# Output projection of a hybrid attention layer: weight blocks split two blocks ahead across products, operand load buffers for each token group, rows of x asked for in products 6 and 4

## The chip, the cores and the metric

The kernel runs on one core of a Trainium2 chip. The metric is the device time of one execution in microseconds (us); lower is better. Times are medians of several runs; a profile is one further execution.

## What is computed

One step of a layer with two groups of heads. A combined input projection feeds stick-breaking attention (8 heads) and retention (8 heads); each branch is normalised by head and gated; both are joined and go through one output projection, and the normalised result is added to the input:

```python
h = rms_norm(x, norm_pre)
q_sb, k_sb, v_sb, gate_sb, q_r, k_r, v_r, gate_r = project(h, w_in, pos)
...
y = jnp.concatenate([y_sb, y_r], axis=-1)
out = jnp.einsum('bte,ed->btd', y, w_out)
xp = xp + rms_norm(out, norm_post)
```

There are 1024 prompt tokens and 8 x 16 = 128 sample tokens, a model width of 2048 and weights w_out of 2048 x 2048, all in float32. The change concerns only the last part, the product y w_out, its normalisation and the addition of x, which fills about the last 395 us.

## The kernel before, in words

**Tiling.** Tokens lie in tiles of 128. Group 0 holds prompt tiles 0 to 3 and the sample tile, group 1 prompt tiles 4 to 7. The output product of a group is done by Strassen's scheme: seven products n, each of a combination of token halves and width halves of y (table LEFT) and one of blocks of w_out (table RIGHT). The order is 5 for group 0 (still in the stage before), then 1, 2, 5 (for group 1 alone), 3, 6, 7, 4. Products 1, 2 and 3 also carry the sample tile in an ordinary product.

**A half product.** Each product has two halves, nh = 0 and 1, of 512 output columns; I call them 1a, 1b and so on. A half (product, L1182) runs over eight blocks k of 128 rows of the weights. Every float32 operand is split in two parts that TensorE takes at full rate: hi is a rounded copy (ScalarE, L162), lo the remainder (VectorE, L163), in the names wh and wl for weights, mh and ml or ah and al for tokens of group 0 and group 1, sh and sl for the sample. A block thus costs three matmuls (hi x hi, hi x lo, lo x hi; L1159, L1162, L1163) for each accumulator: five accumulators in 1, 2 and 3, four in 6, 7 and 4. In 1a the matmuls of group 1 run two blocks behind (LAG). PSUM has eight banks, in a ring; a half takes its four or five from it, the sample's last.

**Loading weights.** load_split (L1174) asks for a block on SyncE's queue into wr (five buffers), and splits it into wh and wl (four buffers each). In the code it stands at the head of iteration k.

**Other work beside the matmuls.** Generators called jobs are advanced by tick(), one step a tick, and a number of ticks follows each group of three matmuls: three for product 1, two for 6 and 7, one otherwise. Jobs are: left (L290), which loads eight pieces of y for each group and splits them into operands of the next product (buffers yr, four, one tag for both groups); left_sample (ys); sums (L271), which loads pieces of y for group 1 (br, two buffers), adds them on VectorE and stores them (s_s, issued by ScalarE); collect (L1206), which copies or adds finished accumulators into the result; complete (L1267), which squares and multiplies by the gain gpost; finish (L1295), which scales four pieces of a finished tile on ScalarE and lets GpSimd's queue add them onto the output rows, which hold x already. The list `then` says in which half the operands of which product are prepared, and they are drained before that product begins.

**The end.** In 4a the eight weight blocks of 4b are also loaded and split, into kept tiles (keep_blocks, L1358). 4b then runs one tile at a time, and its tiles add x themselves: rows of x (128 x 2048, 1 MB) are asked for in load_row (L1369).

**What sets the order.** Each engine runs its instructions in order. The program text gives the order within an engine roughly; a scheduler moves instructions by its own estimate of readiness, except that those that are pinned (pin, L180) may not pass the last matmul written ahead of them. Weight splits are not pinned; the jobs' steps are.

Of the kernel before, what the change touches and what calls it, by code (L numbers as in the profile page):

```python
# [2 lines left out]

# [6 lines left out]
F32 = mybir.dt.float32  # L10
# [6 lines left out]
P = 128  # L17
D = 2048
# [41 lines left out]
D_SUM2 = (4, 6, 36)  # L60
D_SUM3 = (2, 3, 6)
LAG = 2
HT = KT // 2
HALF = D // 2
KEPT = 5
D_KEEP = 2
# [21 lines left out]
def tile_hybrid_step(  # L88
# [27 lines left out]
    nc = tc.nc  # L116
# [12 lines left out]
    def x_rows(t):  # L129
        return x_prompt[0, t * P : (t + 1) * P, :] if t < PT else xs_flat  # L130
# [99 lines left out]
    def drain(job):  # L230
        while job is not None and not job.done:
            tick()
# [57 lines left out]
    def left(gi, n, hi, lo, bufs, tag, deep):  # L290
        src = LEFT[n]
        raw = []

        def load(h):
            r = bufs.tile([P, 256], F32, name=tag, tag=tag, bufs=deep)
            if src[0] == "y":
                pin(nc.sync.dma_start(r, s_y[gi][src[1] * H + h][:, src[2] * 256 : src[2] * 256 + 256]))
            else:
                pin(nc.sync.dma_start(r, s_s[gi][h][:, src[1], :]))
            raw.append(r)  # L300

        for h in range(deep - 1):
            load(h)
        yield D_OP
        for h in range(HT):
            if h + deep - 1 < HT:
                load(h + deep - 1)
            r = raw.pop(0)
            pin(*split(hi[h], lo[h], r))
            yield D_OP  # L310
# [125 lines left out]
    with ExitStack() as s1:  # L436
# [737 lines left out]
        def load_split(n, nh, k):  # L1174
            wr = wp.tile([P, 512], F32, name="wr3", tag="wr", bufs=5)
            nc.sync.dma_start(wr, weights_of(n, nh, k))
            wh = wp.tile([P, 512], F32R, name="wh3", tag="wh")
            wl = wp.tile([P, 512], F32R, name="wl3", tag="wl")
            split(wh, wl, wr)
            return wh, wl  # L1180

        def product(n, nh, groups, sample, ticks, upto=HT, feed=(), lag=0):  # L1182
            todo = [((g, p), bank(), mine[g, n], TS[p]) for g in groups for p in range(2)]
            if sample:
                todo.insert(2, ("s", bank(), mine["s", SAMPLE_LEFT[n]], TS[0]))
            blocks = []
            for k in range(upto + lag):
                if k < upto:
                    blocks.append(load_split(n, nh, k))
                next(iter(feed), None)  # L1190
                for key, a, x, ts in todo:
                    at = k - lag if key[0] == 1 else k
                    if 0 <= at < upto:
                        times(a, x, at, ts, *blocks[at], at == 0, at == HT - 1)
                        for _ in range(ticks):
                            tick()
            return [(key, a) for key, a, _, _ in todo]
# [40 lines left out]
    with ExitStack() as s3:  # L1238
# [18 lines left out]
        def tile_of(key):  # L1257
            return SAMPLE if key[1] == 4 else GROUPS[key[0]]["tiles"][key[1]]
# [48 lines left out]
        def both(n, groups):  # L1307
            made = []
            for g in groups:
                mine[g, n] = operand(c3, ("ah", "al"), 256, bufs=2) if g else kept(at[n])  # L1310
                made.append(left(g, n, *mine[g, n], rp, "yr", 4))
            return made

        def jobs_of(made):
# [2 lines left out]
        def all_of(made):  # L1317
# [5 lines left out]
            (1, 1): ((2, BOTH),), (2, 1): ((5, G1), (3, G0)), (5, 0): ((3, G1),), (3, 0): ((6, BOTH),),  # L1323
            (6, 0): ((7, BOTH),), (7, 0): ((4, BOTH),),
        }
        (first,) = both(1, G1)
        more = Job(sums(fp, [sum_rows(1, h) for h in range(H)], D_SUM3), 16)
        Job(load_gpost(), 40)
# [3 lines left out]
        for n, groups in ((1, BOTH), (2, BOTH), (5, G1), (3, BOTH), (6, BOTH), (7, BOTH)):  # L1332
            for nh in range(2):
                if n > 1 and nh == 0:
                    all_of(ready)
                    ready = []
                if (n, nh) == (2, 1):
                    drain(more)
                for what in then.get((n, nh), ()):
                    ready += jobs_of(both(*what))  # L1340
                start = dict(feed=first, lag=LAG) if (n, nh) == (1, 0) else {}
                accs = product(n, nh, groups, n < 4, {1: 3, 6: 2, 7: 2}.get(n, 1), **start)
                if (n, nh) == (2, 1):
                    phases.close()
                    xp.append(s3.enter_context(tc.tile_pool(name="xp", bufs=1)))
                Job(collect(n, nh, accs), 1)
# [2 lines left out]
        at_end = [half[1].rearrange("p a n -> p (a n)").rearrange("p (k n) -> p k n", k=KEPT) for half in mov]  # L1349
        rest = [mp.tile([P, HT - KEPT, 512], F32R, name=f"w{t}", tag=t) for t in ("mh2", "ml2")]  # L1350
        keep = [[x[:, k] for k in range(KEPT)] + [y[:, k] for k in range(HT - KEPT)] for x, y in zip(at_end, rest)]
        LAST = ((0, 0), (0, 1), (1, 0), (1, 1))
        rows = {
            key: pool.tile([P, D], F32, name=f"x{i}", tag=tag)
            for i, (key, pool, tag) in enumerate(zip(LAST, (rp, rp, xp[0], xp[0]), ("out0", "out1", "x2", "x3")))
        }

        def keep_blocks():  # L1358
            for k in range(HT):
                wr = wp.tile([P, 512], F32, name="wr3", tag="wr", bufs=5)  # L1360
                pin(nc.sync.dma_start(wr, weights_of(4, 1, k)))
                yield 1
                pin(*split(keep[0][k], keep[1][k], wr))
                yield D_KEEP
            for key in LAST[:2]:
                load_row(key)
                yield D_KEEP

        def load_row(key):  # L1369
            pin(nc.sync.dma_start(rows[key], x_rows(tile_of((key[0], 2 + key[1])))))  # L1370

        keeping = Job(keep_blocks(), 1)
        Job(collect(4, 0, product(4, 0, BOTH, False, 2)), 1)
# [1 line left out]
        scaled = [c3.tile([P, 2, 512], F32, name=f"og{t}", tag=t) for t in ("sh", "sl")]  # L1375
        for g, p in LAST:
            key = g, 2 + p
            if g == 0:
                load_row((1, p))
            a = bank()  # L1380
            for k in range(HT):
                times(a, mine[g, 4], k, TS[p], keep[0][k], keep[1][k], k == 0, k == HT - 1, k == 0)
                if (g, p) == (0, 0):
                    tick()
                    tick()
            if (g, p) == (0, 0):
                while jobs:
                    tick()
            o = area(key, 1)
            nc.vector.tensor_tensor(o, o, a, ALU.subtract)  # L1390
            square(key, 1, o)
            t = scaled[g][:, p, :]
            nc.vector.tensor_tensor(t, o, gpost[:, 512:1024], ALU.mult)
            rs = scale(key)
            for c in (0, 2, 3, 1):
                part = t if c == 1 else area(key, c)
                if c or (g, p) == (1, 1):
                    x = rows[g, p][:, c * 512 : (c + 1) * 512]
                    nc.vector.scalar_tensor_tensor(part, part, rs, x, ALU.mult, ALU.add)
                    store(key, c, nc.sync, part)  # L1400
                else:
                    nc.scalar.activation(part, part, AF.Copy, scale=rs)
                    add_out(key, c)
# [104 lines left out]
```

## Time and profile before

| | |
|---|---|
| median of 3 runs | 2335.07 us (2333.79 to 2336.39) |
| profiled execution, whole | 2337.12 us |
| its span, first to last instruction | 2335.4 us |
| granted TensorE clock, mean | 0.992 |
| halves 1a to 4a | 1977.9 to 2303.5 us |
| 4b, one tile after another | 2303.5 to 2325.3 us |

A row of the timeline gives the start in us, the length in us, the engine, the line, the operation with output and inputs, and in brackets how long the engine had been idle and what released it. A row of waits gives who waited for what, the total in us, how often, and the longest. In the rows all accumulators are called a.

### The profile page before, as it was taken

To read this page: it belongs to the slowest core of one execution; us is meant where nothing else is said; L and a number is where in the kernel's file an instruction comes from. 1 tells how busy PE (TensorE), PEld (TensorE's weight loads), DVE (VectorE), ACT (ScalarE), POOL (GpSimd) and SP (SyncE) were. 2 spreads that over 40 slices of the span, in tenths; PEclk is the share of its full clock that TensorE was granted. 3 is DMA by queue.
4 is the path that set the end of the run, shared out by engine and by line. 5 is a ranking of instruction groups with operands and counts; after the bars stand their busy time and mean duration, and the time that the engine had idled before them with its cause. 6 is when DMAs were issued, how large, how long until landed. Compare 5 with 4: busy or idle time off the path is not lost.

```text
span 2335.4 us, 39299 instructions
## 1 busy us (share of the span) xinstructions
PE 2273.8 (97%) x14496; PEld 2050.2 (88%) x14496; DVE 1234.1 (53%) x2541; ACT 920.5 (39%) x1951; POOL 356.9 (15%) x601
## 2 busy tenths in 40 slices
PE   7999999999999999999999999999999999899997
PEld 7999999999999999998888979888889887688775
DVE  7234444353435444355556565655665666545565
ACT  6323333333333333334343334333343445335362
POOL 3002020110202020111111202020220221000020
PEclk9999999999999999999999999999999999999999
DMA  7546657575557647577678787777876767835585
GB/s 253 175 147 201 192 151 218 177 208 172 172 173 206 196 150 220 177 203 253 163 235 213 229 223 229 225 211 228 237 226 204 209 171 200 273 126 168 140 181 189
DMA packets 446497, 462.61 MB, mean 198 GB/s; under 512 B 181984, under 2 KB 309984, under 8 KB 444640
## 3 DMA queue, kind: packets, MB, share of 16 engines
q1 hardware_dynamic: 315952, 295.69, 43.5%
q0 software_dynamic: 28720, 78.41, 11.9%
q10 hardware_dynamic: 101632, 86.00, 11.7%
q8 instruction: 113, 1.85, 0.3%
q14 instruction: 80, 0.66, 0.1%
HBM read 355.12 MB, written 114.29 MB: 201 GB/s over the span
## 4 chain that ended last, share of the span: by engine, by line
PE 83%; DMA 8%; DVE 5%; ACT 2%; issue 2%; SPq 1%; POOL 0%; DVEq 0%; ACTq 0%; POOLq 0%
PE acc L366 46%; PE accn L422 17%; PE a L1162 3%; PE a L1159 3%; PE a L1163 3%; PE pa L747 2%; PE z L717 2%; PE pd L850 1%; PE zc L786 1%; DMA mr<-s_h 1%; DMA yr<-s_y 1%; DMA ro<-s_rk 1%; DMA wr<-s_b 1%; DMA yr<-s_s 1%; DVE wl L163 1%
## 5 line engine op out<-in xcount | busy, mean ns | idle before, releaser
L366 PE MATMUL acc<-mh,wh 128*128 128x256 f32 (+2 forms) x2304 | 663.1, 340 | 0.0
L366 PE MATMUL acc<-ml,wh 128*128 128x256 f32 (+2 forms) x2304 | 659.3, 339 | 0.0
L366 PE MATMUL acc<-mh,wl 128*128 128x256 f32 (+2 forms) x2304 | 656.9, 338 | 0.0
L163 DVE TENSOR_TENSOR wl<-wr,wh 128x512 fp32r<-128x512 f32 x504 | 345.9, 690 | 495.8 <-ACT wh L162 463.7
L162 ACT ACTIVATE wh<-wr 128x512 fp32r<-128x512 f32 x504 | 316.5, 630 | 632.8 <-PE acc L366 342.5
L366 PEld LDWEIGHTS acc<-ml,wh 128*128 128x128 f32 x2304 | 421.7, 188 | 31.4 <-issue 3.3
L366 PEld LDWEIGHTS acc<-mh,wl 128*128 128x128 f32 x2304 | 424.2, 188 | 27.6
L366 PEld LDWEIGHTS acc<-mh,wh 128*128 128x128 f32 x2304 | 420.1, 188 | 31.5 <-issue 3.3
L422 PE MATMUL accn<-whn,mh 128*128 128x256 f32 x1152 | 331.2, 287 | 0.9 <-DVE rg L449 0.8
L422 PE MATMUL accn<-wln,mh 128*128 128x256 f32 x1152 | 327.2, 284 | 0.0
L422 PE MATMUL accn<-whn,ml 128*128 128x256 f32 x1152 | 326.7, 284 | 0.0
L422 PEld LDWEIGHTS accn<-whn,mh 128*128 128x128 f32 x1152 | 221.9, 193 | 4.2 <-DVE rg L449 1.1
L422 PEld LDWEIGHTS accn<-wln,mh 128*128 128x128 f32 x1152 | 222.0, 193 | 0.8
L422 PEld LDWEIGHTS accn<-whn,ml 128*128 128x128 f32 x1152 | 221.7, 193 | 0.0
L163 DVE TENSOR_TENSOR wln<-wrn,whn 128x512 fp32r<-128x512 f32 x128 | 87.6, 688 | 148.2 <-ACT whn L162 146.8
L162 ACT ACTIVATE whn<-wrn 128x512 fp32r<-128x512 f32 x128 | 80.6, 633 | 187.5 <-PE accn L422 93.8
L610 POOL DMA_DIRECT2D be<-s_be x128 | 94.1, 742 | 145.0 <-DMA s_be<-be 121.6
L646 DVE TENSOR_TENSOR_SCAN kp<-kp 128x1152 f32<-128x1152 f32 (+4 forms) x40 | 82.7, 2067 | 51.8 <-POOL kp L635 35.1
L1162 PE MATMUL a<-wl,mh 128*128 128x512 f32 x240 | 96.6, 403 | 7.2 <-DVE wl L163 7.2
L1159 PE MATMUL a<-wh,mh 128*128 128x512 f32 x240 | 95.1, 401 | 7.1 <-ACT wh L162 6.3
L635 POOL TENSOR_SCALAR_AFFINE_SELECT kb<-kb 128x128 f32<-128x128 f32 x64 | 30.6, 485 | 457.6 <-ACT kb L629 455.3
L773 POOL DMA_DIRECT2D kcT<-cache_k x64 | 34.6, 545 | 423.8 <-PE pd L850 268.8
(259 smaller groups left out, 3015.7 us busy)
## 6 DMA issues: line engine op xcount, KB each, us to landing
wr<-w_cols SPq DMA_DIRECT2D x384, 256.0 KB, 4.4
wrn<-w_rows SPq DMA_DIRECT2D x128, 256.0 KB, 3.4
kcT<-cache_k POOLq DMA_DIRECT2D x64, 512.0 KB, 8.3
vc<-cache_v SPq DMA_DIRECT2D x64, 512.0 KB, 5.5
wr<-s_b SPq DMA_DIRECT2D x80, 256.0 KB, 3.7
br<-w_out SPq DMA_DIRECT2D x64, 256.0 KB, 5.2
s_b<-br ACTq DMA_DIRECT2D x32, 512.0 KB, 4.9
wr<-w_out SPq DMA_DIRECT2D x48, 256.0 KB, 3.8
```

The lines of the kernel that those rows point to most:

```text
L162: nc.scalar.activation(hi, src, AF.Copy),
L163: nc.vector.tensor_tensor(lo, src, hi.bitcast(F32), ALU.subtract),
L366: last = nc.tensor.matmul(a[:, :m], lhs[:, j, :], rhs[w][:, j, o : o + m], start=(w == 0 and j == 0 and n == 0), stop=(w == KT // WQ - 1 a ...
L422: anchor[0] = nc.tensor.matmul(a, lhs[q][:, jj, ts], rhs[:, j, :], start=(w == 0 and j == 0 and n == 0 and t % 2 == 0), stop=(w == KT // 2 ...
L610: q.dma_start(raw[32 * i : 32 * i + 32, :].rearrange("p (k a) -> p k a", a=32), s[:, :, 32 * i : 32 * i + 32].rearrange("k (j b) a -> b (k ...
L646: nc.vector.tensor_tensor_scan(rev, rev, rev, 1.0, ALU.mult, ALU.bypass)
L717: nc.tensor.matmul(z[:, :c], q2[a][:, i * P : (i + 1) * P], k2[b][:, s : s + c], start=(m == 0), stop=(m == 2),)
L747: nc.tensor.matmul(po[:, :P], at[:, j, :], vn[:, j, :], start=(j == 0), stop=(j == t))
L773: ready.append((kc, nc.gpsimd.dma_start(kc, cache_k[h, m // 4, m % 4])))
L1159: ins = nc.tensor.matmul(a, hi[k][:, ts], wh, start=first, stop=False)
L1162: nc.tensor.matmul(a, hi[k][:, ts], wl, start=False, stop=False)
L1163: anchor[0] = nc.tensor.matmul(a, lo[k][:, ts], wh, start=False, stop=last)
```

## The change

1. The weight blocks of all halves are put in one sequence (order_of). At iteration k the code now asks for and splits blocks until three stand ready, the one that is used and two more (AHEAD = 2), also across the end of a half. The buffers of wr, wh and wl are as many as before.
2. The pieces of y for group 0 and group 1 have a tag of their own (yr0, yr1) with four buffers each.
3. Ticks: two for each group of matmuls in product 1 (three before), one in product 6 (two before).
4. Rows of x: two of the four are asked for by a job that starts in 6a (steps 8 ticks and 30 more after), into buffers that nothing else needs. The third is asked for behind the last kept block, the fourth after 4a's code, into buffers of finished tiles.

```diff
-                made.append(left(g, n, *mine[g, n], rp, "yr", 4))
+                made.append(left(g, n, *mine[g, n], rp, f"yr{g}", 4))
...
+        made = collections.deque()
+        order_of = iter([(n, nh, k) for n in (5, 1, 2, 5, 3, 6, 7) for nh in range(2) for k in range(HT)] + [(4, 0, k) for k in range(HT)])
...
                 if k < upto:
-                    blocks.append(load_split(n, nh, k))
+                    made.extend(load_split(*at) for at in itertools.islice(order_of, AHEAD + 1 - len(made)))
+                    blocks.append(made.popleft())
...
+        def load_row(key):
+            i = LAST.index(key)
+            pool, tag = ((xp[0], "x0"), (xp[0], "x1"), (rp, "out0"), (rp, "out1"))[i]
+            rows[key] = pool.tile([P, D], F32, name=f"x{i}", tag=tag)
+            pin(nc.sync.dma_start(rows[key], x_rows(tile_of((key[0], 2 + key[1])))))
+
+        def early_rows():
+            for key in LAST[:2]:
+                load_row(key)
+                yield 30
...
+                if (n, nh) == (6, 0):
+                    Job(early_rows(), 8)
...
-                accs = product(n, nh, groups, n < 4, {1: 3, 6: 2, 7: 2}.get(n, 1), **start)
+                accs = product(n, nh, groups, n < 4, {1: 2, 7: 2}.get(n, 1), **start)
...
-            for key in LAST[:2]:
-                load_row(key)
-                yield D_KEEP
+            load_row(LAST[2])
...
-            if g == 0:
-                load_row((1, p))
+            if (g, p) == LAST[0]:
+                load_row(LAST[3])
```

The order of instructions that comes of it, at three places. First VectorE at the beginning of 6b. Before, wl_23379 and wl_23398 are blocks 2 and 3 of 6b; L1218, L1220 and L1271 collect 6a:

```order
L163 TENSOR_TENSOR wl_23379<-wr_23376,wh_23378 128x512
L1218 TENSOR_TENSOR mh_21203<-mh_21203,a_23077 128x512
L1218 TENSOR_TENSOR ml_21204<-ml_21204,a_23078 128x512
L1220 TENSOR_TENSOR mh_21201<-mh_21201,mh_21203 128x512
L1220 TENSOR_TENSOR ml_21202<-ml_21202,ml_21204 128x512
L1218 TENSOR_TENSOR out_21398<-out_21398,a_23079 128x512
L1218 TENSOR_TENSOR out_21399<-out_21399,a_23080 128x512
L1271 TENSOR_TENSOR mh_21201<-mh_21201,gpost 128x512
L1220 TENSOR_TENSOR out_21396<-out_21396,out_21398 128x512
L1271 TENSOR_TENSOR ml_21202<-ml_21202,gpost 128x512
L1220 TENSOR_TENSOR out_21397<-out_21397,out_21399 128x512
L1271 TENSOR_TENSOR out_21396<-out_21396,gpost 128x512
```

The next row is `L163 TENSOR_TENSOR wl_23398<-wr_23395,wh_23397 128x512`. Now wl_23333, wl_23356 and wl_23380 are blocks 2, 3 and 4 of 6b:

```order
L166 TENSOR_TENSOR wl_23333<-wr_23330,wh_23332 128x512
L166 TENSOR_TENSOR ml_12223<-yr_23246,mh_12222 128x256
L1225 TENSOR_TENSOR mh_21215<-mh_21215,a_23089 128x512
L166 TENSOR_TENSOR al<-yr_23253,ah 128x256
L1227 TENSOR_TENSOR mh_21213<-mh_21213,mh_21215 128x512
L1225 TENSOR_TENSOR ml_21216<-ml_21216,a_23090 128x512
L166 TENSOR_TENSOR wl_23356<-wr_23353,wh_23355 128x512
L1227 TENSOR_TENSOR ml_21214<-ml_21214,ml_21216 128x512
L1225 TENSOR_TENSOR out_21410<-out_21410,a_23091 128x512
L1225 TENSOR_TENSOR out_21411<-out_21411,a_23092 128x512
L1227 TENSOR_TENSOR out_21408<-out_21408,out_21410 128x512
L166 TENSOR_TENSOR wl_23380<-wr_23377,wh_23379 128x512
```

The eleven operations that stood between two weight splits are now cut by the split of block 3 after five and by that of block 4 after four more.

Second, ScalarE at the end of 1b. Before, s_s1_7 is the last of the eight stores, wh3_21957, wh3_21983 and wh3_22005 are blocks 0, 1 and 2 of 2a, and L1216 copies the accumulators of 1b:

```order
L286 DMA s_s1_7_134<-br_21732 128x1024
L162 ACTIVATE ah_21691<-yr_21771 128x256
L162 ACTIVATE wh3_21957<-wr3_21955 128x512
L162 ACTIVATE mh0_12124<-yr_21776 128x256
L162 ACTIVATE ah_21691<-yr_21784 128x256
L162 ACTIVATE mh0_12124<-yr_21792 128x256
L162 ACTIVATE ah_21691<-yr_21796 128x256
L162 ACTIVATE wh3_21983<-wr3_21981 128x512
L162 ACTIVATE wh3_22005<-wr3_22003 128x512
L1216 ACTIVATE mh3_21203<-a3_21693 128x512
L1216 ACTIVATE ml3_21204<-a3_21694 128x512
```

Now wh3_21887 is block 7 of 1b, and wh3_21914, wh3_21938 and wh3_21968 are blocks 0 to 2 of 2a:

```order
L165 ACTIVATE ah_21686<-yr1_21808 128x256
L165 ACTIVATE wh3_21887<-wr3_21885 128x512
L165 ACTIVATE wh3_21914<-wr3_21912 128x512
L289 DMA s_s1_5_132<-br_21771 128x1024
L165 ACTIVATE wh3_21938<-wr3_21936 128x512
L289 DMA s_s1_6_133<-br_21857 128x1024
L165 ACTIVATE wh3_21968<-wr3_21966 128x512
L1223 ACTIVATE mh3_21215<-a3_21688 128x512
L1223 ACTIVATE ml3_21216<-a3_21689 128x512
```

The operand splits (ah, mh0) have all moved ahead of block 7 of 1b; the sixth and seventh store have moved in between, and the eighth follows the copies.

Third, SyncE's queue near the end of 4a. Before, L1361 are the kept blocks and L1176 those of 4a; wr_24125, wr_24143 and wr_24161 are its blocks 5, 6 and 7:

```order
L1361 DMA wr_24113<-s_b_7_118 128x512
L1176 DMA wr_24125<-s_b_5_108 128x512
L1370 DMA x_23973<-x_prompt 128x2048
L1370 DMA x_23974<-x_prompt 128x2048
L1176 DMA wr_24143<-s_b_6_109 128x512
L1176 DMA wr_24161<-s_b_7_110 128x512
L1370 DMA x_23975<-x_prompt 128x2048
L1370 DMA x_23976<-x_prompt 128x2048
```

Now wr_24111 and wr_24137 are blocks 6 and 7 of 4a, L1378 the kept blocks:

```order
L1378 DMA wr_24091<-s_b_4_115 128x512
L1378 DMA wr_24102<-s_b_5_116 128x512
L1378 DMA wr_24109<-s_b_6_117 128x512
L1179 DMA wr_24111<-s_b_6_109 128x512
L1378 DMA wr_24125<-s_b_7_118 128x512
L1340 DMA x_24132<-x_prompt 128x2048
L1179 DMA wr_24137<-s_b_7_110 128x512
L1340 DMA x_24181<-x_prompt 128x2048
```

One row of x stands ahead of the last block instead of two ahead of the last two; the other two are now in this queue directly behind the first weight blocks of 6b and of 7a.

More of the change, by code (lines that the diff above doesn't have):

```diff
@@ L1 @@
+import collections
+import itertools
 import math
@@ L62 @@
 LAG = 2
+AHEAD = 2
 HT = KT // 2
@@ L1325, in tile_hybrid_step @@
         }
+        LAST = ((0, 0), (0, 1), (1, 0), (1, 1))
+        rows = {}
+        def load_row(key):
[7 more added lines that the diff above has]
+                yield 30
         (first,) = both(1, G1)
@@ L1351, in tile_hybrid_step @@
         keep = [[x[:, k] for k in range(KEPT)] + [y[:, k] for k in range(HT - KEPT)] for x, y in zip(at_end, rest)]
[L1352 to L1356, printed above, removed]
         def keep_blocks():
@@ L1364, in keep_blocks @@
                 yield D_KEEP
-            for key in LAST[:2]:
-                load_row(key)
-                yield D_KEEP
-        def load_row(key):
-            pin(nc.sync.dma_start(rows[key], x_rows(tile_of((key[0], 2 + key[1])))))
+            load_row(LAST[2])
         keeping = Job(keep_blocks(), 1)
```

## The prediction

> **What bounds the kernel now.** I read the page's busy line first and then asked for the busy time of every half product of the output stage. Product n has halves a and b; T is the time at which TensorE starts a half. The windows below are, in order, 1a, 1b, 2a, 2b, 6a, 6b, 7a, 7b and 4a; the columns are length, PE, PE weight loads, DVE, ACT, POOL, granted clock, DMA share and GB/s.
>
> ```profile
> PE 2273.8 (97%) x14496; PEld 2050.2 (88%) x14496; DVE 1234.1 (53%) x2541; ACT 920.5 (39%) x1951; POOL 356.9 (15%) x601
> ...
> 1977.93:2009.40 31.47, 29.39 (x121) 23.45 (x120) 17.73 (x44) 13.36 (x33) 2.19 (x4) 0.95 0.88 291
> 2009.40:2037.65 28.25, 27.81 (x121) 22.38 (x120) 15.03 (x35) 8.55 (x21) 0.00 (x0) 1.00 0.81 264
> 2037.65:2071.40 33.75, 28.96 (x121) 23.47 (x120) 10.98 (x20) 9.55 (x18) 0.00 (x0) 0.95 0.33 112
> 2071.40:2098.60 27.20, 27.20 (x121) 22.54 (x120) 17.07 (x35) 13.57 (x34) 0.00 (x0) 1.00 0.50 157
> ...
> 2174.77:2196.53 21.76, 21.76 (x97) 18.03 (x96) 12.45 (x31) 12.07 (x28) 3.54 (x4) 1.00 0.78 199
> 2196.53:2222.02 25.49, 23.68 (x97) 19.08 (x96) 15.27 (x26) 8.98 (x19) 0.00 (x0) 0.93 0.36 111
> 2222.02:2243.77 21.75, 21.75 (x97) 18.02 (x96) 17.14 (x47) 15.41 (x37) 3.50 (x4) 1.00 0.81 206
> 2243.77:2271.56 27.79, 24.94 (x97) 20.05 (x96) 15.15 (x39) 14.31 (x29) 10.57 (x12) 0.88 1.07 204
> 2271.56:2303.49 31.93, 24.93 (x97) 18.73 (x96) 17.04 (x28) 12.41 (x26) 0.00 (x0) 0.95 0.62 217
> ```
>
> A half with 120 weight loads (one per matmul) takes 27.20 us when PE never stops (2b), one with 96 takes 21.76 us (6a). So a block of weights is worth 27.20/8 = 3.40 us or 21.76/8 = 2.72 us of PE. What each half takes beyond that is the whole field of this change: 1a 4.27, 1b 1.05, 2a 6.55, 6b 3.73, 7b 6.03, 4a 10.17, together **31.8 us**. The kernel is bound by TensorE, and outside these halves nothing here can be won.
>
> The waits of PE after 1980 us name who was late: the second split wl (DVE) six times, the first one wh (ACT) four times, and once the copy ml of a finished accumulator (ACT).
>
> ```profile
> PE a L1162 <- DVE wl L163: 7.2, 6, 2.8
> PE a L1159 <- ACT wh L162: 6.3, 4, 2.8
> PE a L1159 <- ACT ml L1216: 4.8, 1, 4.8
> PE a L1159 <- ACT ah L162: 0.6, 1, 0.6
> ```
>
> These add to 18.9 us, not 31.8. The rest stands in the spacing of the matmuls after a wait, as in 6b:
>
> ```profile
> 2204.70 0.39 PE L1159 MATMUL a<-wh,mh 128*128 128x512 f32 x1
> 2206.90 0.50 PE L1162 MATMUL a<-wl,mh 128*128 128x512 f32 x1 [1.81 <-DVE wl L163]
> ...
> 2208.30 0.63 PE L1163 MATMUL a<-wh,ml 128*128 128x512 f32 x1
> 2208.72 0.63 PE L1159 MATMUL a<-wh,ah 128*128 128x512 f32 x1
> ```
>
> The starts are 0.42 us apart after the gap (2208.30 to 2208.72) and 0.227 (27.20/120) at full rate; the window of 6b shows a clock of 0.93. A gap of 2.20 us so cost 3.73. The Trainium skill (TensorE: Matmul & The Clock Gate, "What's actually happening") says that the array falls to half rate after an idle window of about 3.4 us. Taken as a bound on gaps it would leave 6b with about 2.0 us of excess; this gap was shorter and the rate still fell, so the row decides.
>
> **The change part by part.** *Splits two blocks ahead (6b, 7b, 4a).* In 6b the splits of block 3 stood on DVE behind the additions that collect 6a:
>
> ```profile
> 2198.34 1.29 DVE L163 TENSOR_TENSOR wl<-wr,wh 128x512 fp32r<-128x512 f32 x2
> 2199.55 0.68 DVE L1218 TENSOR_TENSOR mh<-mh,a 128x512 f32<-128x512 f32 x1
> 2200.15 0.68 DVE L1218 TENSOR_TENSOR ml<-ml,a 128x512 f32<-128x512 f32 x1
> ...
> 2205.55 0.69 DVE L1271 TENSOR_TENSOR out<-out,gpost 128x512 f32<-128x512 f32 x1
> 2206.15 0.69 DVE L163 TENSOR_TENSOR wl<-wr,wh 128x512 fp32r<-128x512 f32 x1
> ```
>
> Eleven additions and products at 0.60 us each (2199.55 to 2200.15) put wl at 2206.15, while PE had its wh at 2204.70. In the changed order only five operations (three of 0.60, two halves of about 0.42) stand between the wl of blocks 2 and 3, and four more before block 4. The earliest that the split of block 3 can run is T, since wh has four buffers and block 7 of 6a must leave. From T - 2 the five take 2.6 us, wh 0.62 and wl 0.69, so it is done before T + 3.5; PE needs it at T + 3 x 2.72 = T + 8.2. Nothing else becomes late: **-3.7 us**. In 7b the wl of block 2 likewise moves from behind ten such operations of the collecting to behind three; it is ready at about T - 1.8 + 3 x 0.6 + 0.7 and some short ones, T + 1.5, and needed at T + 5.4: **-6.0 us**. In 4a blocks 0 to 2 are now split ahead of the collecting of 7b. Block 3 follows twelve operations, T - 1.8 + 12 x 0.6 + 0.7 = T + 6.1, and is needed at T + 8.2.
>
> *Rows of x (4a, 6, 7).* The later stalls of 4a are loads. The requests on SP, the waits of ACT, and the times to landing between 2270 and 2300 us (size, median):
>
> ```profile
> 2282.59 0.32 SPq L1176 DMA_DIRECT2D wr<-s_b  x1
> 2283.08 0.83 SPq L1370 DMA_DIRECT2D x<-x_prompt  x2
> 2284.01 1.97 SPq L1176 DMA_DIRECT2D wr<-s_b  x2
> ```
>
> ```profile
> 2289.70 0.63 ACT L162 ACTIVATE wh<-wr 128x512 fp32r<-128x512 f32 x1 [3.76 <-DMA wr<-s_b]
> 2295.52 0.63 ACT L162 ACTIVATE wh<-wr 128x512 fp32r<-128x512 f32 x1 [5.19 <-DMA wr<-s_b]
> ```
>
> ```profile
> x<-x_prompt SPq DMA_DIRECT2D x4, 1024.0 KB, 12.2
> wr<-s_b SPq DMA_DIRECT2D x10, 256.0 KB, 3.5
> ```
>
> Block 5, asked for at 2282.59 just ahead of 2 MB of x, came after 7.1 us; block 6, just behind them, after 11.5; an undisturbed one takes 3.5. Now two of the four rows are loaded in 6 and 7, and on SP only one of 1 MB stands ahead of the last weight block, the other behind it. Block 6 has no x ahead. By the ring of five wr buffers the request of block 7 follows the split of kept block 4, whose own request follows the split of block 3: T + 6.1, 3.5 to land, 0.6 and 0.7 for the split, T + 11 or a little more. The row ahead of it waits until GpSimd has added a finished tile to the output; behind it on SP stands block 7. POOL is busy 10.57 us in 7b and not at all in 4a, so that wait should be over. For 1 MB ahead of it I take the middle between 3.5 and 11.5, 7.5 us: landed T + 18.8, split T + 19.4, needed at T + 19.0 (7 x 2.72). With some of that on block 6 and the slow matmuls that follow a gap, I leave 4a 1.8 us; the ends are 0 (3.5 us) and 4 + 2 = 6 us (11.5). So **-8.4 us**. The Trainium skill (DMA: Bandwidth & Descriptors, "Queues, rings and completion order") says that an engine takes descriptors in ring order. By that alone block 7 would wait for the 1 MB ahead and not for the row behind, and 4a would keep under 1 us; block 5, slowed to 7.1 us with x asked for only behind it, speaks against so clean an order.
>
> The x row of 6 costs SP 0.8 us at most and the transfers 1.05 MB/291 GB/s (the rate of 1a) = 3.6 us. Behind it in SP's order stand operand loads, whose waiting ACT then has wh behind them. In 6 and 7 the split of block k may run four blocks, 10.9 us, ahead of its use, which covers 3.6; the DMA share in 6b is 0.36. I take 0, with 0 to 3.6 as bounds.
>
> *Operand buffers and slower ticks (1a, 1b, 2a).* At the start of 2a, the sample's accumulator takes the bank that the second copy of 1b frees, and that copy waited on ACT behind operand splits, and these on loads:
>
> ```profile
> 2036.93 0.40 ACT L162 ACTIVATE mh<-yr 128x256 fp32r<-128x256 f32 x1
> 2040.35 0.42 ACT L162 ACTIVATE ah<-yr 128x256 fp32r<-128x256 f32 x1 [3.02 <-DMA yr<-s_y]
> ...
> 2042.90 0.57 ACT L1216 ACTIVATE mh<-a 128x512 f32<-128x512 f32 x1
> 2043.38 1.07 ACT L1216 ACTIVATE ml<-a 128x512 f32<-128x512 f32 x2
> ```
>
> ```profile
> L286 ACTq DMA_DIRECT2D s_s<-br x8: 326/326/327, 1990.9 to 2034.4; - x8
> ```
>
> With four buffers per group the sixteen operand splits stand wholly ahead of the last block of 1b. What now stands ahead of the copies is the seventh store s_s. Eight were issued in 43.5 us, 6.2 apart, the first 13.0 us after the start of 1a. The new pace, 17 steps an item at ten per 3.40 us, is 5.8 us and does not bind. The seventh comes near 13 + 6 x 6.2 = 50 us, and 2a starts at 2 x 27.2 = 54.4 or later: covered by some 4 us. I leave 0.5 us: **-6.0 us**; the ends are 0 and all 6.55. In 1a PE waited at 1993.83 to 1995.67 for a wh of ACT that stood behind splits of the sample's rows (ys):
>
> ```profile
> 1994.79 0.31 ACT L162 ACTIVATE sh<-ys 128x128 fp32r<-128x128 f32 x1 [1.82 <-DMA ys<-s_y]
> 1995.00 0.61 ACT L162 ACTIVATE wh<-wr 128x512 fp32r<-128x512 f32 x1
> ...
> 1998.18 0.31 ACT L162 ACTIVATE sh<-ys 128x128 fp32r<-128x128 f32 x1 [2.26 <-DMA ys<-s_y]
> ```
>
> That block (5) is now ahead of all eight; block 6 is behind four and block 7 behind eight. If the rows land as now, the last after 21 us, block 7 is split at 22.5 and needed at 21.1. I leave 1a 2.0 us (ends 0 and 4.27) and 1b 0.5 of its 1.05: **-2.8 us**.
>
> The sum is 3.7 + 6.0 + 8.4 + 6.0 + 2.8 = **26.9 us**. The profiled execution took 2337.1 us with a span of 2335.4; the median of the runs is 2335.1, 2 us below it, and I take the sum from the median: **2308 us**.
>
> **Rivals.** *Traffic keeps the first half* (0.2): 1a and 1b run at DMA shares of 0.88 and 0.81, the same bytes must move, and 1a, 1b and 2a keep their 11.9 us. Against it: the stalls there are places in ACT's order, and 2a itself has a share of 0.33. Gain 18.1, 2317 us.
>
> *x takes its own place again* (0.1): the row in 6 and the one ahead of the last block hold loads as in 4a. 4a keeps 6 and 6a or 6b pays 3.6: 26.9 - 4.2 - 3.6 = 19.1, 2316 us.
>
> *The early splits do not come early* (0.05): wl placed first waits for PE to leave a buffer anyway. Then 6b, 7b and the first 3 us of 4a stay: 26.9 - 12.7 = 14, 2321 us. The changed order speaks against it.
>
> *Slower* (0.04): a wl placed ahead of the collecting makes DVE, which runs in order, wait for PE; the copies free the sample's bank late, and each half with five accumulators (1b, 2a, 2b, 3a, 3b) stops as 2a does now, 6.55 us. That decides once the copy is over 1.36 us (six matmuls) behind T. Four new such stops cost 26.2 and 2a gains nothing, 26.9 - 6.0 - 26.2 = -5.3, 2340 us. Against it: for 2b, 3a and 3b the order on DVE is nearly that of before, and 2b took 27.20.
>
> **How the numbers follow.** The forecast has 0.61. Its own range is 2303 (all 31.8 gone) to 2314. The range 2303 to 2320 takes in the first two rivals. A measurement of this kernel can tell about 0.2%, 4.7 us; all cases but the last are far beyond, and I keep a little for losses that I don't see: faster 0.92, same 0.03, slower 0.05.
>
> **What would show it.** Six halves at 27.2 or 21.8 us show each term right: 6b and 7b above 23 show the splits still late, with DVE wl as releaser; 4a above 25 with ACT idle for a wr load shows x; 2a above 29 with an ACT copy as releaser, behind s_s, shows the stores; 1a above 30 the ys rows. I am wrong if 6a, 7a or 3a, now at full rate, grow.

## The result, and the profile after

The changed kernel took 2319.42 us (median of 5 runs, 2316.21 to 2322.67); the kernel before, beside it on the same chip, 2333.79 (5 runs, 2327.26 to 2336.39). The ratio is 0.9946 with a 95% interval of 0.9924 to 0.9968: about 12.6 us faster, where 26.9 were forecast. A second series gave 0.9919 (0.9895 to 0.9944), about 19 us. The profiled execution took 2318.99 us with a span of 2317.3.

The busy line of the page, and then the same nine windows as in the prediction (1a, 1b, 2a, 2b, 6a, 6b, 7a, 7b, 4a) with the columns length, PE, PE weight loads, DVE, ACT, POOL, clock, DMA share, GB/s:

```profile
PE 2265.7 (98%) x14496; PEld 2046.9 (88%) x14496; DVE 1231.3 (53%) x2541; ACT 919.1 (40%) x1951; POOL 358.1 (15%) x601
```

```profile
1979.14:2015.26 36.12, 29.61 (x121) 23.45 (x120) 16.98 (x43) 13.14 (x32) 2.18 (x4) 0.95 0.78 248
2015.26:2043.88 28.62, 28.62 (x121) 23.51 (x120) 16.00 (x39) 13.69 (x30) 0.00 (x0) 0.95 0.85 279
2043.88:2071.08 27.20, 27.20 (x121) 22.52 (x120) 10.00 (x18) 5.67 (x10) 0.00 (x0) 1.00 0.40 129
2071.08:2098.29 27.21, 27.21 (x121) 22.52 (x120) 16.83 (x35) 13.05 (x34) 0.00 (x0) 1.00 0.50 157
2174.45:2196.21 21.76, 21.76 (x97) 18.02 (x96) 13.94 (x35) 11.91 (x29) 1.48 (x2) 1.00 0.82 240
2196.21:2217.96 21.75, 21.75 (x97) 18.02 (x96) 13.30 (x23) 8.86 (x18) 2.07 (x3) 1.00 0.78 184
2217.96:2239.72 21.76, 21.76 (x97) 18.02 (x96) 19.48 (x54) 17.70 (x42) 5.47 (x8) 1.00 0.89 220
2239.72:2261.48 21.76, 21.76 (x97) 18.02 (x96) 13.35 (x32) 12.59 (x27) 8.60 (x10) 1.00 1.07 218
2261.48:2285.41 23.93, 22.06 (x97) 17.94 (x96) 15.54 (x26) 10.61 (x22) 0.00 (x0) 1.00 0.75 229
```

Four of the six halves did as forecast: 2a is 27.20 (33.75 before), 6b 21.75 (25.49), 7b 21.76 (27.79), 4a 23.93 (31.93). Together they give 24.3 us. But **1a grew from 31.47 to 36.12**, and 1b from 28.25 to 28.62: 5.0 us are lost where 2.8 were to be won. The rest of the difference of the two spans (18.1) is 1.2 us by which the profile after comes later into 1a, in code that both kernels share. The waits of PE from 1975 us on now name four places only, and the two largest are in 1a:

```profile
PE a L1166 <- DVE al L166: 3.7, 1, 3.7
PE a L1162 <- ACT ah L165: 2.6, 1, 2.6
PE a L1162 <- ACT wh L165: 1.9, 1, 1.9
PE a L1165 <- DVE wl L166: 0.2, 1, 0.2
```

Stalls are given below from the start of one matmul to the start of the next.

**The first stall of 1a** (1985.05 to 1988.07) waits for the first operand split of group 1, ah. What led to it starts on VectorE, with the last attention output of the stage before: kT turns it, sg multiplies it, and ScalarE's queue stores sg to s_y. Before, the two stand together; after, the wl of a weight block is between them. VectorE before, then after (start, length, operation, idle time and what ended it):

```profile
1977.38 0.71 DVE L680 STREAM_TRANSPOSE kT<-so 128x512 f32<-128x512 f32 x1
1978.12 0.75 DVE L681 SCALAR_TENSOR_TENSOR sg<-kT,gains,sg 128x512 f32<-128x512 f32 x1
```

```profile
1978.59 0.71 DVE L683 STREAM_TRANSPOSE kT<-so 128x512 f32<-128x512 f32 x1
1981.09 0.69 DVE L166 TENSOR_TENSOR wl<-wr,wh 128x512 fp32r<-128x512 f32 x1 [1.80 <-ACT wh L165]
1981.70 0.74 DVE L684 SCALAR_TENSOR_TENSOR sg<-kT,gains,sg 128x512 f32<-128x512 f32 x1
```

That wl waits for its wh, which on ScalarE stands behind the five copies of the accumulators of product 5. ScalarE after, then before:

```profile
1977.99 1.09 ACT L1223 ACTIVATE mh<-a 128x512 f32<-128x512 f32 x2
1978.96 1.59 ACT L1223 ACTIVATE ml<-a 128x512 f32<-128x512 f32 x3
1980.39 0.67 ACT L165 ACTIVATE wh<-wr 128x512 fp32r<-128x512 f32 x1
...
1982.48 0.35 ACTq L687 DMA_DIRECT2D s_y<-sg  x1
1987.60 1.03 ACT L165 ACTIVATE ah<-yr 128x256 fp32r<-128x256 f32 x3 [5.93 <-DMA br<-s_y]
```

```profile
1978.90 0.33 ACTq L684 DMA_DIRECT2D s_y<-sg  x1
...
1982.00 1.03 ACT L162 ACTIVATE ah<-yr 128x256 fp32r<-128x256 f32 x3 [1.54 <-DMA yr<-s_y]
```

So sg starts 2.55 us after the start of 1a (1979.15) and not 0.18 (1977.94), and its store leaves later by as much. It also takes longer (size, us to landing; before, then after):

```profile
s_y<-sg ACTq DMA_DIRECT2D x1, 256.0 KB, 2.8
```

```profile
s_y<-sg ACTq DMA_DIRECT2D x1, 256.0 KB, 4.9
```

It lands at 1982.48 + 4.9 = 1987.4, and ah starts at 1987.60, though the yr rows that it reads were asked for from 1979.43 on and take 3.3 us (median) to land. The page puts this wait down to br; but ah is a tile of a pool that opens when those of the stage before close, and this one instruction waits for twelve DMA queues and GpSimd, the next ah for one queue. The trace also tells which of the twelve came last: ScalarE passed the waits for the first eight by 1983.1, that for the queue of sg's store at 1987.44, just after the landing, and the rest at once. The split ahead of sg is to be seen in the changed order, on VectorE near the start of 1a, a place of which the prediction says nothing:

```
L683 STREAM_TRANSPOSE kT<-so 128x512
L166 TENSOR_TENSOR wl_21441<-wr_21438,wh_21440 128x512
L684 SCALAR_TENSOR_TENSOR sg<-kT,gains,sg 128x512
```

**The second stall** (2010.69 to 2014.74) waits for al of the last block. Its ah is done in time, but on VectorE al stands behind a sum (br<-br) that waits for its own load, and the wl of a later block:

```profile
2009.38 0.40 ACT L165 ACTIVATE ah<-yr 128x256 fp32r<-128x256 f32 x1
```

```profile
2007.89 0.69 DVE L1225 TENSOR_TENSOR mh<-mh,a 128x512 f32<-128x512 f32 x1 [0.43 <-ACT mh L1223]
2013.32 0.43 DVE L286 TENSOR_TENSOR br<-br 128x256 f32<-128x256 f32 x1 [4.74 <-DMA br<-s_y]
2013.66 0.68 DVE L166 TENSOR_TENSOR wl<-wr,wh 128x512 fp32r<-128x512 f32 x1
2014.27 0.42 DVE L166 TENSOR_TENSOR al<-yr,ah 128x256 fp32r<-128x256 f32 x1
```

VectorE stood still for 4.74 us with work behind it whose data was there.

### The profile page after: what moved, and what is told of

The parts are those of the page before. It is cut to its first block, busy times and chain, and to the rows that moved or that the text cites. A ratio compares the mean times of both kernels' runs of the same rounds, so it can differ in the third digit from the quotient of the medians.

```text
span 2317.3 us, 39306 instructions
## 1 busy us (share of the span) xinstructions
PE 2265.7 (98%) x14496; PEld 2046.9 (88%) x14496; DVE 1231.3 (53%) x2541; ACT 919.1 (40%) x1951; POOL 358.1 (15%) x601
## 4 chain that ended last, share of the span: by engine, by line
PE 85%; DMA 7%; DVE 4%; issue 2%; ACT 2%; SPq 0%; POOL 0%; DVEq 0%; ACTq 0%; POOLq 0%
PE acc L369 46%; PE accn L425 17%; PE a L1166 4%; PE a L1162 4%; PE a L1165 4%; PE pa L750 2%; PE z L720 2%; PE zc L789 1%; PE pd L853 1%; DMA mr<-s_h 1%; DMA s_o<-so 1%; PE pa L898 1%; DVE ml L166 1%; PE pS L913 1%; PE rs L880 1%
## 5 line engine op out<-in xcount | busy, mean ns | idle before, releaser
L1166 PE MATMUL a<-wh,ml 128*128 128x512 f32 x240 | 94.0, 392 | 0.0
```

The source lines that it names most:

```text
L1166: anchor[0] = nc.tensor.matmul(a, lo[k][:, ts], wh, start=False, stop=last)
```

## The experiments

In all that follows, the excess of a half is the time from its first matmul to the first of the next half, less 0.2267 us for each of its matmuls. All from profiles of one execution; halves that are not listed (2b, 5a to 6a, 7a) had none in any kernel. The medians come from four series of runs, in which the kernel before took 2333.8 to 2338.3, so that only the ratios compare across rows; beside the second profile of before stands the median of its series.

| kernel | 1a | 1b | 2a | 6b | 7b | 4a | sum | median of runs, us | ratio to before (95%) |
|---|---|---|---|---|---|---|---|---|---|
| before | 4.3 | 1.0 | 6.5 | 3.7 | 6.0 | 10.2 | 31.7 | 2333.8 | |
| before, second profile | 4.6 | 1.5 | 5.5 | 2.0 | 4.9 | 9.8 | 28.3 | 2334.7 | |
| after | 8.9 | 1.4 | 0 | 0 | 0 | 2.2 | 12.5 | 2319.4 | 0.9946 (0.9924 to 0.9968) |
| after, second profile | 8.9 | 0.1 | 0 | 0 | 0 | 2.2 | 11.2 | 2317.3 | 0.9919 (0.9895 to 0.9944) |
| after, steps 3 in product 1 | 6.8 | 0.9 | 0 | 0 | 0 | 1.9 | 9.7 | 2317.1 | 0.9918 (0.9895 to 0.9941) |
| after, no look-ahead | 7.8 | 1.4 | 0 | 0 | 0 | 3.8 | 13.0 | 2319.5 | 0.9926 (0.9904 to 0.9948) |
| before + look-ahead | 6.3 | 0 | 5.4 | 0.1 | 0 | 9.7 | 21.5 | 2327.8 | 0.9960 (0.9947 to 0.9973) |
| before + buffers | 5.1 | 1.1 | 0 | 0 | 0 | 9.4 | 15.6 | 2320.1 | 0.9936 (0.9914 to 0.9957) |
| before + steps | 7.9 | 1.2 | 0 | 0 | 5.9 | 10.9 | 25.9 | 2329.5 | 0.9982 (0.9970 to 0.9994) |
| before + x rows | 5.7 | 0 | 7.3 | 7.4 | 6.7 | 4.5 | 31.5 | 2333.6 | 0.9999 (0.9983 to 1.0014) |
| after, splits tied | 5.8 | 0 | 0.7 | 0 | 0 | 1.8 | 8.3 | 2319.8 | 0.9941 (0.9922 to 0.9960) |
| the same, steps 3 | 2.6 | 3.5 | 0 | 0 | 0 | 1.8 | 7.9 | 2317.3 | 0.9929 (0.9914 to 0.9943) |
| after, sums later | 4.4 | 0 | 0 | 0 | 0 | 3.7 | 8.1 | 2312.5 | 0.9907 (0.9890 to 0.9923) |
| after, tied and sums later | 0.3 | 0 | 0 | 0 | 0 | 2.1 | 2.4 | 2311.4 | 0.9900 (0.9883 to 0.9916) |

**The changed kernel again.**

> The changed kernel unaltered, to see how far its first half 1a (36.12 us, 8.9 above full rate) belongs to the kernel and not to one execution. Theory L (loads): the weight blocks asked for two ahead fill the queues as 1a starts and the operand rows land late. Theory P (pace): two steps for each accumulator instead of three put sums on VectorE ahead of an operand split that TensorE waits for. By either, the order of the instructions makes the loss and 1a is 35 to 37 us again, 2316 to 2323 us in all. Rival R (luck): loads land late in some executions and not in others; then 1a is anywhere from 29 to 37, and the time moves with it.

1a took 36.16 us, with the same two stalls (3.49 ahead of ah, 3.57 ahead of al). The loss belongs to the kernel; luck as its cause falls.

**Three steps in product 1 again.**

```diff
-{1: 2, 7: 2}.get(n, 1)
+{1: 3, 7: 2}.get(n, 1)
```

> Product 1 back to three steps for each accumulator; all else of the change stays. Theory P: the stall of 4.05 us ahead of the last block of 1a (al behind the sums on VectorE) goes, 1a is about 32, the time 4 us lower, 2315; 2a keeps its gain, since four buffers for each group bring it. Theory L: the steps only set where the sums stand, the first stall (3.0 us, ah waiting for yr) stays, and 1a stays at 34 to 36. Rival: with three steps the stores of the sums crowd ahead of the copies at 2a again and 2a goes back to 33, time 2321 or more.

1a is 34.06: the stall ahead of al shrank to 1.71 us, that ahead of ah stayed (3.11), and another of 1.71 ahead of wh came in. Fewer steps are part of the second stall's cause and none of the first's. That wh (1.71) stands behind the sample's rows on ScalarE, the wait that the prediction's step meant to remove. 2a stayed at full rate, so the rival on its stores falls.

**No look-ahead.**

```diff
-AHEAD = 2
+AHEAD = 0
```

> The changed kernel without the look-ahead (each weight block asked for and split in its own step); buffers, steps and x rows as changed. Theory L: 1a loses its first stall and is 31.5 to 33; the stalls of 6b (3.7) and 7b (6.0) come back, 4a is 25.7 or more; time 2319 + 9.7 - 3 to 4, 2324 to 2327. Theory P: 1a stays at 36 and the time is 2329 or more.

Both theories missed. The stall ahead of ah is gone, as theory L had it, but 1a took 35.0 us (31.5 to 33 by theory L, 36 by theory P), and 6b and 7b stayed at full rate:

```profile
2192.45:2214.21 21.76, 21.76 (x97) 18.02 (x96) 13.30 (x23) 8.86 (x18) 2.06 (x3) 1.00 0.83 184
...
2235.97:2257.73 21.76, 21.76 (x97) 18.02 (x96) 12.58 (x31) 11.14 (x23) 8.13 (x10) 1.00 1.06 213
```

So the look-ahead causes the first stall of 1a and is not what 6b and 7b needed. What it is good for is seen in 4a (2.2 against 3.8 us): the wait for the wl of block 1, 2.27 us from matmul to matmul, stands in all six profiles without the look-ahead and in none with it. In 1a three waits of 1.7 to 1.9 us come in without it, behind sums and the sample's rows that wait for loads. Beside the other parts it is worth 0.5 to 1.8 us by the sums, and the runs (2317.3 with, 2319.5 without) can't tell that from nothing.

**Look-ahead alone**, on the kernel before.

> The kernel of before with the look-ahead alone: shared operand buffers, three steps, x rows late. Theory L: 6b and 7b at full rate (-9.7), 4a still above 25 because of the x rows, 2a still 33, and 1a up from 31.5 to 34.5; time 10 to 12 below before without 1a's loss, 7 to 9 below with it. Theory P: 1a is 31.5 as before or better, and the time is 10 to 12 us below before.

6b and 7b are at full rate, 2a and 4a are not, and 1a is up by 2.1 us, with a stall of 3.29 us ahead of ah and one of 1.71 ahead of an al. In the code before, too, the look-ahead makes that stall: sg stands behind a wl and starts at 1979.9, 2.6 us into 1a.

**Splits tied.** To tell the bytes of the blocks (L) from their place on VectorE (S), the splits were tied behind the last matmul written ahead of them; the loads are asked for as early as in the changed kernel.

```diff
-            split(wh, wl, wr)
+            pin(*split(wh, wl, wr))
```

> The changed kernel with the splits of the weight blocks tied behind the product's matmuls, so that on VectorE no block split ahead stands between kT and sg, the last two instructions ahead of the last store of the stage before. Theory S (store): in 1a the wl of a block asked for ahead holds sg until ScalarE's five copies are done; sg's store leaves 2.4 us later and lands 5 us later instead of 3, and ah, the first write into memory of the stage before, waits for it. Then sg starts some 0.2 us after the start of 1a instead of 2.55, the stall ahead of the first ah (3.0 us) falls under 0.5, 1a is 33 and the time 3 us lower than the changed kernel's, 2314 to 2316. Theory L (loads): the bytes of the weight blocks make the operand rows late, the stall stays at 3 us, 1a stays at 36.

1a is 33.03 us, 3.1 less, and the stall ahead of ah is gone. On VectorE sg follows kT again, and ah waits for nothing (no bracket):

```profile
1975.57 0.70 DVE L683 STREAM_TRANSPOSE kT<-so 128x512 f32<-128x512 f32 x1
1976.31 0.75 DVE L684 SCALAR_TENSOR_TENSOR sg<-kT,gains,sg 128x512 f32<-128x512 f32 x1
```

```profile
1985.76 1.03 ACT L165 ACTIVATE ah<-yr 128x256 fp32r<-128x256 f32 x3
```

Theory S holds; L as it was put, operand rows that land late, falls. The edit moved more than was meant: sg now starts 5.9 us ahead of 1a, where 0.2 us behind its start was expected, and its store, though it took 5.6 us, had landed 3 us ahead of ah. Where ah did wait, it started 0.1 to 0.3 us after sg's store had landed, whatever else was under way: 1986.04 after 1980.7 + 5.2 (look-ahead alone), 1987.19 after 1982.2 + 4.8 (sums later), 1985.72 after 1980.8 + 4.6 (x rows), 1987.60 after 1987.4 (changed kernel). The x rows' kernel has VectorE's order of before at this place and still had a stall of 1.54 us there. On ScalarE its store stands behind a wh and an mh, which before stood behind the store, and so was issued 1.9 us after sg had started:

```profile
1979.99 0.66 ACT L165 ACTIVATE wh<-wr 128x512 fp32r<-128x512 f32 x1
1980.51 0.45 ACT L165 ACTIVATE mh<-mr 128x256 fp32r<-128x256 f32 x1
1980.82 0.35 ACTq L687 DMA_DIRECT2D s_y<-sg  x1
```

So this wait too is made by an order, on the other engine. The time of the tied kernel, 2319.8 (2314 to 2316 expected), does not show the gain; its ratio lies between the two of the changed kernel. What was left in 1a is the second mechanism at another place, a sum waiting with a wl behind it:

```profile
1995.26 1.80 DVE L286 TENSOR_TENSOR br<-br 128x256 f32<-128x256 f32 x4 [3.97 <-DMA br<-s_y]
1996.98 0.42 DVE L166 TENSOR_TENSOR al<-yr,ah 128x256 fp32r<-128x256 f32 x1
1997.32 0.68 DVE L166 TENSOR_TENSOR wl<-wr,wh 128x512 fp32r<-128x512 f32 x1
```

**Buffers alone**, on the kernel before.

> The kernel before with load buffers for each group alone. The kernel without the look-ahead kept the gains of 6b and 7b, so the look-ahead is not what they need. Theory B (buffers): operand splits that wait for a shared buffer stand on ScalarE ahead of the weight split; with buffers of their own 7b is 21.8 (-6.0), 2a 27.2 (-6.5), 6b 21.8 if not for its steps; time 10 to 16 us below before. Theory of the prediction (look-ahead needed): 6b and 7b stay at 25.5 and 27.8, only 2a gains; time 6.5 below before. 1a as before, 31.5 (both).

2a, 6b and 7b are all at full rate: this one line gives as much as the whole change within what the runs can tell (0.9936 against 0.9946 and 0.9919), and 3 to 4 us less by the sums. How it does so in 6b corrects my reading. VectorE in this kernel, where 6b starts at 2193.24:

```profile
2191.43 0.69 DVE L163 TENSOR_TENSOR wl<-wr,wh 128x512 fp32r<-128x512 f32 x1 [2.03 <-ACT wh L162]
2192.05 0.68 DVE L1218 TENSOR_TENSOR mh<-mh,a 128x512 f32<-128x512 f32 x1
...
2198.05 0.68 DVE L1271 TENSOR_TENSOR out<-out,gpost 128x512 f32<-128x512 f32 x1
2198.65 0.68 DVE L163 TENSOR_TENSOR wl<-wr,wh 128x512 fp32r<-128x512 f32 x1
```

The same eleven operations stand in one row between two weight splits, and cost nothing. The collecting begins 1.2 us ahead of 6b; before, it began 3.0 us into it (2199.55 against 2196.54), because the last operand split ahead of it waited for a row, with weight splits behind it. ScalarE before:

```profile
2197.37 0.42 ACT L162 ACTIVATE ah<-yr 128x256 fp32r<-128x256 f32 x1 [2.36 <-DMA yr<-s_s]
```

So the wl of block 3 started 9.6 us into 6b before, 5.4 with the buffers, and is needed at 8.2.

**Steps alone**, on the kernel before.

> The kernel before with the steps of the changed kernel alone: product 1 two for each accumulator instead of three, product 6 one instead of two. Theory P (pace): 1a gets the stall ahead of its last block's al (2.8 to 4.0 us) that the kernels with two steps showed, and 6b goes to full rate (-3.7); 7b and 2a as before; time from 3 below to 1 above before. Rival: the steps move nothing by themselves, 1a 31.5, 6b 25.5, same time.

6b and 2a go to full rate (the second was expected by neither theory), 7b and 4a keep their stalls, and 1a grows by 3.6 us, with 2.83 ahead of al: theory P's part, in a kernel without look-ahead. The net is 4 us by the runs, close to the end of theory P's range (3 below).

**x rows alone**, on the kernel before.

> The kernel before with the x rows asked for early, alone. The prediction's term: 4a 31.9 to 24 (-8), all else as before, time 8 below before. Rival: the x rows in 6 hold the operand loads of 6 and 7 and 6b or 7b grows by up to 3.6 us; time 4 to 5 below before. Rival 2: in 4a the weight blocks are late without the look-ahead, 4a stays at 25.5 to 27, 5 to 6 below.

4a has 4.5 left of 10.2, and 6b grew to 7.4: the first rival's mechanism, in the kernel with shared operand buffers. At the border of 6b ScalarE waited 6.0 us for a row of y that was asked for just behind a row of x; before, its longest wait there was 2.4 us. The time is not that rival's (4 to 5 below): 6b and smaller growths of 1a, 2a and 7b use up the gain of 4a, and the ratio is 0.9999. Beside buffers of their own the early rows are a gain: 4a goes from 9.4 (buffers alone) to 3.8 (no look-ahead, which has the new steps too; these alone left 4a at 10.9), and 6b is at full rate in both.

**The kernel before again**, for a second profile.

> The kernel before unaltered, for a second profile of it. Its runs so far lie between 2327 and 2344 us, those of the changed kernel between 2314 and 2323. Theory V (varying): the stalls of before differ from execution to execution by their loads, and the first profile (35.2 us above full rate in the output stage, 2337 in all) was one of the slow ones; here the sum is 26 to 35. Rival: the output stage loses the same 35 again, and the spread comes from the stages ahead (the start of 1a has lain between 1976.5 and 1983.3 in the profiles so far).

Its span is 2330.6, its sum 28.3 against 31.7: part of the first profile's loss was that execution. The other part of the spread lies ahead of the change: the first matmul of the output stage came between 1940.3 and 1947.1 us in stages whose program text the change leaves as it was. Both explanations hold.

**Tied, with three steps.**

> The tied kernel with three steps in product 1. Theory Q (queue): what is left of 1a's loss is VectorE standing in a sum (br<-br) that waits for its load, with wl or al behind it; three steps move the sums to other places but leave them in 1a, so 1a stays between 30 and 33 and no stall is ahead of the first ah. Theory P as first put: two steps are the cause of the rest, and 1a is 28 to 29. Time 2312 to 2318.

1a is 29.8 and 1b 30.7: the stalls behind the sums moved on into 1b, where theory Q had left them in 1a (30 to 33). No stall is ahead of ah. What is left in 1a is again a wh (1.58) behind a row of the sample, for which ScalarE waited 5.1 us. Theory Q holds in the main; theory P's 28 to 29 was not reached, and the steps only choose where a waiting sum stands.

**Sums later.**

```diff
-        more = Job(sums(fp, [sum_rows(1, h) for h in range(H)], D_SUM3), 16)
+        more = Job(sums(fp, [sum_rows(1, h) for h in range(H)], D_SUM3), 80)
```

> The changed kernel with the sums of the second group's rows begun 64 steps later, with the start of 1b; nothing else moved. Theory Q: the stall ahead of al (4.05 and 3.57 us in two profiles) goes and the first (3.0 to 3.5, ahead of ah) stays, perhaps shorter, since no br load then runs beside the store of sg; 1a 31 to 32; in 1b only weight splits two blocks ahead stand behind a sum, 1b under 28; time 4 below the changed kernel. Rival: al waits for its own yr load and 1a stays above 35. Rival 2: the sums' stores hold the copies at the start of 2a, and 2a takes 3 or more of it back.

The stall ahead of al is gone, the one ahead of ah stays (2.90), 1a is 31.6, and 1b and 2a are at full rate. The br loads alone are not what makes sg's store slow: here it took 4.8 us without one beside it, though behind two weight loads. 4a has 1.5 us more than in the changed kernel, which nothing in this edit explains.

**Both.**

> The changed kernel with both: splits tied behind the matmuls, and the sums begun with 1b. Theories S and Q together: neither the stall ahead of the first ah nor those behind the sums are left, 1a 27.2 to 28.5, 4a 23.5 to 24 as in the changed kernel; 7 to 8 us below the changed kernel, 2309 to 2312. If only one holds, 1a is 30 to 32.

The windows of 1a and 1b, and all waits of PE behind 1981 us:

```profile
1981.40:2008.89 27.49, 27.48 (x121) 22.45 (x120) 11.94 (x27) 13.40 (x33) 2.19 (x4) 1.00 0.59 187
2008.90:2036.09 27.19, 27.19 (x121) 22.53 (x120) 14.53 (x35) 12.86 (x29) 0.00 (x0) 1.00 0.86 282
```

```profile
PE a L1162 <- ACT wh L165: 1.3, 1, 1.3
PE a L1165 <- DVE wl L166: 0.2, 1, 0.2
```

1a is at full rate but for 0.3 us. The time is 2311.4 us (2308.2 to 2313.2), ratio 0.9900 (0.9883 to 0.9916): 23 us below the kernel before. Its interval lies under that of the changed kernel's first series and overlaps that of the second; by the sums of the profiles it is 8.8 to 10.1 us better than the changed kernel. The tie also changes the order ahead of the output stage: in the three tied kernels its first matmul comes 2.23 us after the one before it, in the others 0.9 to 2.0. What that costs is not shown.

## Why the prediction was right or wrong

**The step that failed is the term of 1a and 1b**, "-2.8". It measured +5.0 in the first pair of profiles, and that 7.8 is all of the difference (7.6) between the sum of 26.9 and the 19.3 that the halves gave. The stall that the step treated, a wh of ScalarE behind the sample's rows, did go: none of PE's waits in 1a after is of that kind. But the step looked only at the wait that was there. Two new ones came: the look-ahead put a weight split ahead of sg (3.0 us; with the slow matmuls after it 3.1 by the tied kernel), and, above all by the fewer steps, al came to stand behind a sum that waits (4.05 us; 4.5 by the kernel with the sums later). The sign that the prediction set, 1a above 30 for the sample's rows, would have named the wrong cause; 3a, 6a and 7a stayed at full rate.

A smaller error is one of size. All terms were read from one profile, and in the second profile of before 2a, 6b, 7b and 4a have 22.2 us to lose and not 26.4. The runs gave 12.6 and 19 us where the one pair of profiles gave 18 in span.

**6b, 7b (-3.7, -6.0): right in size; the cause given is enough but not needed.** I gave both to the look-ahead. It brings both alone, but without it both stay at full rate; the buffers alone bring both too, the steps alone 6b. The row of eleven operations was read rightly, but not what started it late: an operand split waiting for a row in a shared buffer. The prediction costed the buffers in 1a, 1b and 2a only.

**2a (-6.0): right, 6.5.** Buffers or steps each bring it; the look-ahead alone leaves 5.4.

**4a (-8.4): right, 8.0**, with 2.15 left where 1.8 was said. The x rows alone bring 5.7, and the look-ahead 1.6 in the changed kernel. What is left comes with two blocks whose loads are late on both sides of a row of x. SyncE's requests, the last kept block, the row and block 7 of 4a, and ScalarE's waits for the two blocks:

```profile
2272.25 0.32 SPq L1378 DMA_DIRECT2D wr<-s_b  x1
2272.74 0.33 SPq L1340 DMA_DIRECT2D x<-x_prompt  x1
2273.16 0.38 SPq L1179 DMA_DIRECT2D wr<-s_b  x1
```

```profile
2278.63 0.63 ACT L165 ACTIVATE wmh<-wr 128x512 fp32r<-128x512 f32 x1 [2.53 <-DMA wr<-s_b]
2281.88 0.63 ACT L165 ACTIVATE wh<-wr 128x512 fp32r<-128x512 f32 x1 [2.62 <-DMA wr<-s_b]
```

The kept block, asked for ahead of the row, was split 6.4 us after its request, block 7 behind the row 8.7 us after; 7.5 to landing was the estimate. The median of these loads is 4.2. The Trainium skill (DMA: Bandwidth & Descriptors, "Queues, rings and completion order") lets a DMA engine take descriptors in ring order, but adds that a later one may finish its write before an earlier one. The order alone, by the prediction's estimate, would have left under 1 us; the kept block's 6.4 us, like block 5's 7.1 before, show that the order alone does not give the time here.

That the row of x in 6 costs nothing held in the changed kernel, and was 3.7 us too kind for the kernel with shared buffers.

**The rivals.** "Traffic keeps the first half" gave 2317, near the time, for the wrong reason: 2a was won, and 1a after is longer at a DMA share of 0.78 and 248 GB/s, less than before (0.88, 291). In the kernel with both, the br loads leave 1a (share 0.59), which alone would not tell a queue from traffic; but 1b then carries them at a share of 0.86 and 282 GB/s and runs at full rate. "x takes its own place again" was real for one part alone. The slower rival came nearest to what struck, a wl that holds up what stands behind it on VectorE; it looked for it at the accumulators and not at the stage's last store.

**What stays open.** sg's store takes 2.8 to 3.3 us in five profiles and 4.6 to 5.7 in nine; all with the look-ahead are among the nine, but so is the x rows' kernel. The traces show what goes with it: in the five, 512 to 768 KB of loads asked for ahead of the store had not landed when it was issued, in the nine 1024 to 1280 KB, and in twelve of the fourteen profiles the store landed 0.2 to 1.2 us after the last of these loads (in the other two within 0.2 us ahead of it). In the changed kernel the blocks asked for ahead are among these loads. So of the 4.4 us by which ah came later into 1a, 2.4 are sg's place and some 2 the longer store; no experiment changed the loads alone, so this second part is not shown as a cause. Nor is the run series' spread (ratio 0.9946 and 0.9919 for one kernel) explained beyond the 7 us by which the stage's start moves.

## What to carry to other kernels

When work is moved ahead, read in the new order what it is moved ahead of, across the border of the stage too: here one weight split held a store on which the next stage's first write waited. On an engine that runs in order, a load-dependent step of a side job may stall everything behind it, so place it where what follows has slack. And when several edits aim at one stall, take each alone before crediting any: one line of buffers gave nearly the whole gain, and the look-ahead, worth 7 to 10 us by the sums on the kernel before, was worth 0.5 to 1.8 beside it.

## What was not expected of the hardware

The first instruction that wrote into a new stage's pool waited for twelve queues: an ah whose rows had been asked for 8.2 us earlier started 0.2 us after a store had landed that it does not read. The same 256 KB store took 2.8 us where 512 KB of loads asked for before it were still on their way, and up to 5.7 where it was 1024 KB or more.
